# Both MLP products of a tuned fp32 encoder block by one level of Strassen's algorithm

## The chip, the cores and the metric

The kernel runs on one core of one Trainium2 chip. The metric is device microseconds (us) of one execution. The kernel before takes 1759.4 us in the median of three runs (1758.09 to 1764.33). One more execution was recorded by the profiler, and every time below that isn't such a run's comes from that record, counted from the start of its span.

## The reference, cut to what matters

The reference is one layer of an encoder on 1024 tokens of 1024 features: input projection, a state-space mixer, a neighbourhood attention, an output projection, and then the part that the change touches, a squared-ReLU MLP with 4096 hidden features, everything in float32:

```python
x = x + jnp.concatenate([y_ssm, y_na.astype(y_ssm.dtype)], axis=-1) @ w_out
h = rmsnorm(x, norm_mlp_w)
return x + jnp.square(jax.nn.relu(h @ w_mlp_in)) @ w_mlp_out
# x: (1, 1024, 1024), w_mlp_in: (1024, 4096), w_mlp_out: (4096, 1024)
```

## The kernel before

Each float32 product is made of three matmuls on values split in two: a high part, which is the value copied to the matmul's type (ACT), and a low part, the difference from it (a subtraction on POOL or DVE). `mm3` (lines 176 to 179) issues high times high, high times low and low times high into one PSUM tile. `load_w` (lines 133 to 150) loads 128 x 1024 elements of a weight (`wraw`, 512 KB, issued on SP), copies the high part `wh` on ACT (line 147) and subtracts the low part `wl` (line 148) on the engine it is given: POOL everywhere in the MLP. `split_from_psum` (lines 181 to 188) does the same for what comes out of PSUM, on ACT (line 183) and DVE (line 184).

The stages follow one another: projections with the mixer, the attention with the output projection mixed into it, then the MLP (line 968 on). The attention stage ends in the last products of the output projection, whose sums `po` DVE adds into `x2` (line 795). `x2`, 8 tiles of 128 tokens x 1024, lies in SBUF throughout.

The MLP begins with the norm of each token tile t: a square and sum on ACT (line 983), the root on POOL (lines 200 and 201), the scaled tile `hn` on DVE (line 985), eight 128 x 128 transposes on PE (line 209), and the split into `h2h` and `h2l`. `hn` has two buffers, so tile t waits for the transposes of t-2. Then 8 blocks `fb` of 512 hidden features. In a block, 4 columns j by 2 token halves h sum 8 parts k by three matmuls (192 of 128x512); each sum goes through relu (ACT, line 1011), square (DVE, 1012), and a split into `ah` (ACT, 1013) and `al` (DVE, 1014), which stay in SBUF. The block's part of the second product follows at once: 2 halves of the output by 8 token tiles by 4 parts by three matmuls (192 again), each sum added into `x2` on DVE (line 1024). In the last block each finished 128 x 512 piece goes out by DMA (line 1026).

The order on each engine comes from a scheduler that places instructions by estimated times when the program is built; each engine then works through its own list in that order, and an instruction that waits holds what stands behind it on its engine. DMAs are issued from such a list too (SP's).

## Time and profile before

| | us |
|---|---|
| runs, median (lowest to highest) | 1759.4 (1758.09 to 1764.33) |
| profiled execution, its span | 1754.2 |
| median of the runs less that span | 5.2 |
| PE busy in the span | 1695.5 (97%) |
| DVE, ACT, POOL busy | 948.8 (54%), 601.9 (34%), 555.1 (32%) |
| first matmul of the MLP, end of the last add | 1050.47, 1751.07 |

PE is TensorE's matmul stream, DVE VectorE, ACT ScalarE, POOL GpSimd and SP the engine that issues most DMAs. Busy time of PE is no measure of one matmul here, since matmuls overlap in its pipeline: the distance between starts is. The MLP takes the last 700 us of the span.

### The profile page before, as it was taken

To read this page: it belongs to the slowest core of one execution; us is meant where nothing else is said; L and a number is where in the kernel's file an instruction comes from. 1 tells how busy PE (TensorE), PEld (TensorE's weight loads), DVE (VectorE), ACT (ScalarE), POOL (GpSimd) and SP (SyncE) were. 2 spreads that over 40 slices of the span, in tenths; PEclk is the share of its full clock that TensorE was granted. 3 is DMA by queue.
4 is the path that set the end of the run, shared out by engine and by line. 5 is a ranking of instruction groups with operands and counts; after the bars stand their busy time and mean duration, and the time that the engine had idled before them with its cause. 6 is when DMAs were issued, how large, how long until landed. Compare 5 with 4: busy or idle time off the path is not lost.

```text
span 1754.2 us, 20790 instructions
## 1 busy us (share of the span) xinstructions
PE 1695.5 (97%) x7789; PEld 1368.8 (78%) x7789; DVE 948.8 (54%) x1601; ACT 601.9 (34%) x1079; POOL 555.1 (32%) x448
## 2 busy tenths in 40 slices
PE   6999999999898999999999999999999999999999
PEld 5788887777676777777777788888888888888887
DVE  4767115889787744787787745333333333333232
ACT  5434223334334433555565434131212121212120
POOL 4000005787788722220243124121212121212110
PEclk9999999999999999999999999999999999999999
DMA  8114239867676796563562112121212121212102
GB/s 208 49 39 121 72 97 259 205 177 225 200 211 180 230 286 208 190 192 94 167 205 85 49 48 84 49 60 37 61 37 60 37 61 37 60 37 60 37 13 96
DMA packets 176448, 202.63 MB, mean 116 GB/s; under 512 B 11915, under 2 KB 119387, under 8 KB 176347
## 3 DMA queue, kind: packets, MB, share of 16 engines
q1 hardware_dynamic: 133371, 164.07, 31.9%
q10 hardware_dynamic: 42976, 37.23, 7.0%
q8 instruction: 62, 1.02, 0.2%
q14 instruction: 39, 0.32, 0.1%
HBM read 151.66 MB, written 52.94 MB: 117 GB/s over the span
## 4 chain that ended last, share of the span: by engine, by line
PE 74%; DMA 7%; DVE 6%; POOL 6%; issue 4%; ACT 1%; SPq 1%; ACTq 0%; POOLq 0%; DVEq 0%
PE pm L178 13%; PE pm L179 13%; PE pm L177 13%; PE po L177 4%; PE po L179 3%; PE po L178 3%; PE pv L867 3%; PE px L177 3%; PE px L178 3%; PE px L179 3%; DMA rb<-cum_dr 2%; PE psc L893 2%; PE ptp L921 2%; POOL rb L611 2%; PE pz L179 2%
## 5 line engine op out<-in xcount | busy, mean ns | idle before, releaser
L148 POOL TENSOR_TENSOR wl<-wraw,wh 128x1024 fp32r<-128x1024 f32 x84 | 202.6, 2424 | 626.0 <-ACT wh L147 626.0
L147 ACT ACTIVATE wh<-wraw 128x1024 fp32r<-128x1024 f32 x124 | 131.1, 1059 | 407.8 <-PE pm L179 250.8
L1024 DVE TENSOR_TENSOR x<-x,pm 128x512 f32<-128x512 f32 x128 | 87.9, 687 | 230.8 <-PE pm L179 230.0
L178 PE MATMUL pm<-h2l,wh 128*128 128x512 f32 x512 | 199.4, 389 | 0.2 <-DVE h2l L184 0.2
L177 PE MATMUL pm<-h2h,wh 128*128 128x512 f32 x512 | 199.4, 389 | 0.0
L179 PE MATMUL pm<-h2h,wl 128*128 128x512 f32 x512 | 199.2, 389 | 0.0
L178 PE MATMUL pm<-wl,ah 128*128 128x512 f32 x512 | 199.2, 389 | 0.0
L179 PE MATMUL pm<-wh,al 128*128 128x512 f32 x512 | 199.2, 389 | 0.0
L177 PE MATMUL pm<-wh,ah 128*128 128x512 f32 x512 | 199.2, 389 | 0.0
L1012 DVE TENSOR_TENSOR r<-r 128x512 f32<-128x512 f32 x64 | 98.4, 1539 | 182.3 <-ACT r L1011 182.3
L178 PE MATMUL pq<-wl,hTh 128*128 128x512 f32 x384 | 153.5, 401 | 5.0 <-DVE wl L148 5.0
L177 PE MATMUL pq<-wh,hTh 128*128 128x512 f32 x384 | 154.7, 405 | 1.3 <-ACT wh L147 1.3
L179 PE MATMUL pq<-wh,hTl 128*128 128x512 f32 x384 | 153.1, 400 | 0.0
L178 PEld LDWEIGHTS pm<-h2l,wh 128*128 128x128 f32 x512 | 96.1, 188 | 20.5 <-DVE h2l L184 0.5
L177 PEld LDWEIGHTS pm<-wh,ah 128*128 128x128 f32 x512 | 96.1, 188 | 20.0
L177 PEld LDWEIGHTS pm<-h2h,wh 128*128 128x128 f32 x512 | 96.1, 188 | 19.9
L178 PEld LDWEIGHTS pm<-wl,ah 128*128 128x128 f32 x512 | 96.1, 188 | 19.9
L179 PEld LDWEIGHTS pm<-wh,al 128*128 128x128 f32 x512 | 96.1, 188 | 19.9
L179 PEld LDWEIGHTS pm<-h2h,wl 128*128 128x128 f32 x512 | 96.1, 188 | 19.8
L148 DVE TENSOR_TENSOR wl<-wraw,wh 128x1024 fp32r<-128x1024 f32 x40 | 55.1, 1382 | 80.0 <-ACT wh L147 79.3
L183 ACT ACTIVATE pth<-ptp 128x384 fp32r<-128x384 f32 (+1 forms) x128 | 58.5, 459 | 107.3 <-PE ptp L921 106.4
L178 PEld LDWEIGHTS pq<-wl,hTh 128*128 128x128 f32 x384 | 74.1, 193 | 22.3 <-DVE wl L148 7.6
(215 smaller groups left out, 3500.1 us busy)
## 6 DMA issues: line engine op xcount, KB each, us to landing
wraw<-in_w_in_dram SPq DMA_DIRECT2D x44, 512.0 KB, 4.3
rb<-cum_dr SPq DMA_DIRECT2D x32, 512.0 KB, 7.0
wraw<-in_w_mlp_in_dram SPq DMA_DIRECT2D x32, 512.0 KB, 4.2
wraw<-in_w_mlp_out_dram SPq DMA_DIRECT2D x32, 512.0 KB
q_dr<-hl ACTq DMA_DIRECT2D x64, 128.0 KB, 4.0
k_dr<-hl ACTq DMA_DIRECT2D x16, 512.0 KB, 3.2
v_dr<-hl ACTq DMA_DIRECT2D x16, 512.0 KB, 2.6
q<-q_dr SPq DMA_DIRECT2D x8, 1024.0 KB, 7.1
```

The lines of the kernel that those rows point to most:

```text
L147: nc.scalar.activation(hi[:, 0:n], raw[:, 0:n], AF.Copy)
L148: lo_eng.tensor_tensor(lo[:, 0:n], raw[:, 0:n], hi[:, 0:n].bitcast(F32), op=sub)
L177: nc.tensor.matmul(pt, lhsT=ah, rhs=bh, start=first, stop=False)
L178: nc.tensor.matmul(pt, lhsT=ah, rhs=bl, start=False, stop=False)
L179: return nc.tensor.matmul(pt, lhsT=al, rhs=bh, start=False, stop=last)
L183: nc.scalar.activation(hi, src, AF.Copy)
L611: nc.gpsimd.tensor_tensor(rb[:, d], rb[:, d], c1[:, d, c, h0 : h0 + 4].unsqueeze(2).broadcast_to([P, 4, P]), op=sub,)
L867: pvm = nc.tensor.matmul(pv[i][:, (c0 - 4 * i) * P : (c1 - 4 * i) * P], lhsT=v[:, g, hh], rhs=pt[:, g, c0 - g + 1 : c1 - g + 1, :], start= ...
L893: mark = nc.tensor.matmul(pt[:, 0:n], lhsT=q[hp, hh, qs], rhs=kl[hp, ks], start=False, stop=True)
L921: nc.tensor.transpose(pp[:, s], pr[:, s], ident)
L1012: nc.vector.tensor_tensor(r, r, r, op=mul)
L1024: nc.vector.tensor_tensor(d, d, pt, op=add)
```

## The change

Strassen's algorithm (Winograd's form) multiplies two matrices cut into 2 x 2 quarters with seven products of quarters for eight, at the price of sums and differences of quarters before and after. Here both MLP products are done so, and the MLP falls into two stages.

Stage 1 (8 blocks of 512 hidden features): the weight block is loaded in four quarters, combined on DVE (`s1w`, `s2w`, two differences) and split as before into `wh` and `wl` (ACT and POOL). The normed activations are combined once, at the stage's start (`b11` to `b22`, DVE on 2048 columns, then split into `hh` and `hl`). Seven products of 24 matmuls each, in the order 1, 2, 6, 5, 7, 3, 4, make the quarters `c11` to `c22` in SBUF, partly by ACT copies out of PSUM and partly by DVE adds; relu and square are on ACT. The seven combinations that the second product needs (`s1`, `s2`, `s4` among them) are stored to HBM as `act_dr`. `x2` is stored to HBM too.

Stage 2 (4 blocks of 1024 hidden features): weights are loaded, combined and split, the stored combinations are loaded (`ar`), split (`ah` on ACT, `al` on DVE), and seven products of 48 matmuls per block are added into `acc`, which is loaded from the stored `x2`.

The new functions `chain` (three matmuls, as `mm3`), `split_to` and `ring_tile` (buffers in a ring) are in the diff, which is cut to its core:

```diff
+    def split_to(hl, src, eng):
+        nc.scalar.activation(hl[0], src, AF.Copy)
+        eng.tensor_tensor(hl[1], src, hl[0].bitcast(F32), op=sub)
...
+        raws, hls = [wp] * 2 + [wq] * 6, [wp] * 3
...
             for t in range(NT):
                 xt = x2[:, t, :]
+                nc.sync.dma_start(x2_dr[t], xt)
...
                 nc.vector.scalar_tensor_tensor(hn, xt, r, wb, op0=mul, op1=mul)
-                transpose_split(h2h, h2l, t, hn)
...
+                    if i:
+                        split_from_psum(hc[i][0][s], hc[i][1][s], pv)
+                    nc.scalar.copy(xq[g, t // 4][s], pv)
...
+        def h_sub(out, a, b, i, eng):
+            nc.vector.tensor_tensor(out, a, b, op=sub)
+            if i:
+                hc_tiles(hB, i)
+                split_to(hc[i], out, eng)
+
+        b11, b12, b21, b22 = xq[0, 0], xq[0, 1], xq[1, 0], xq[1, 1]
+        h_sub(b11, b12, b11, None, None)
+        h_sub(b12, b22, b12, None, None)
+        h_sub(b22, b22, b11, 6, nc.vector)
+        hc_tiles(hB, 5)
+        split_to(hc[5], b11, nc.gpsimd)
+        hc_tiles(hB, 7)
+        split_to(hc[7], b12, nc.vector)
+        h_sub(b21, b21, b22, 4, nc.gpsimd)
...
+            for i in ORD:
+                if i == 1:
+                    w[1] = w_split(a11, nc.gpsimd)
+                    w[2] = w_split(a12, nc.gpsimd)
+                    s1w, s2w = raw_tile(), raw_tile()
+                    nc.vector.tensor_tensor(s1w, a21, a22, op=add)
+                    nc.vector.tensor_tensor(s2w, s1w, a11, op=sub)
+                    nc.vector.tensor_tensor(a21, a11, a21, op=sub)
+                elif i == 6:
+                    w[6] = w_split(s2w, nc.gpsimd)
+                    nc.vector.tensor_tensor(a12, a12, s2w, op=sub)
...
+                    if i in (1, 6, 5):
+                        nc.scalar.copy({1: c11, 6: c12, 5: c22}[i][:, j], pt)
+                    elif i == 4:
+                        nc.scalar.activation(c21[:, j], pt, AF.Relu)
+                    else:
+                        c = {2: c11, 7: c22, 3: c12}[i][:, j]
+                        nc.vector.tensor_tensor(c, c, pt, op=add)
...
+                elif i == 4:
+                    nc.scalar.activation(c21, c21, AF.Square)
+                    store(2, c21)
+                    nc.vector.tensor_tensor(s4, c21, s2, op=sub)
+                    store(3, s4)
...
+        raws, hls = [wp] * 2 + [wy] * 10, [wp] * 3 + [wy] * 3
...
+        def a_split(fb, i, u):
+            ar = ap2.tile([P, 1024], F32, tag="ar", name="ar", bufs=4)
+            nc.sync.dma_start(
+                ar.rearrange("p (a t) -> p a t", a=2), act_dr[fb, i - 1, :, 2 * u : 2 * u + 2, :]
+            )
+            hl = [ap2.tile([P, 1024], F32R, tag=n, name=n, bufs=5) for n in ("ah", "al")]
+            split_to(hl, ar, nc.vector)
+            return hl
...
+            for i in ORD:
+                wa = []
+                for u in range(2):
+                    q = bq[u]
+                    if i == 6:
+                        q["t1"], q["t2"] = raw_tile(), raw_tile()
+                        nc.vector.tensor_tensor(q["t1"], q["12"], q["11"], op=sub)
+                        nc.vector.tensor_tensor(q["t2"], q["22"], q["t1"], op=sub)
+                        nc.vector.tensor_tensor(q["12"], q["22"], q["12"], op=sub)
+                    elif i == 4:
+                        nc.vector.tensor_tensor(q["21"], q["21"], q["t2"], op=sub)
+                    src = q[{1: "11", 2: "21", 3: "22", 4: "21", 5: "t1", 6: "t2", 7: "12"}[i]]
+                    wa.append((a_split(fb, i, u), w_split(src, nc.gpsimd)))
...
+                    nc.vector.tensor_tensor(d, d, pt, op=add)
+                    if fb == 3 and i in (2, 7, 3, 4):
                         nc.sync.dma_start(
```

Up to the MLP the two programs issue the same instructions in the same order on every engine. PE's list is 384 matmuls shorter: 1344 in each stage, 2688 in all, for 3072.

The first place is DVE's list at the MLP's start. Before, the norm (`hn`, line 985) and the splits of the transposed tiles (`h2l`, line 184) are all that stands between the output projection's adds and the first block's squares:

```order
L985 SCALAR_TENSOR_TENSOR hn<-x_5436,r_9127,wb_9038 128x1024
L795 TENSOR_TENSOR x_5436<-x_5436,po 128x512
L184 TENSOR_TENSOR h2l<-ptn,h2h 128x4x128 x4
L985 SCALAR_TENSOR_TENSOR hn<-x_5436,r_9148,wb_9038 128x1024
L985 SCALAR_TENSOR_TENSOR hn<-x_5436,r_9169,wb_9038 128x1024
L184 TENSOR_TENSOR h2l<-ptn,h2h 128x4x128 x2
L985 SCALAR_TENSOR_TENSOR hn<-x_5436,r_9190,wb_9038 128x1024
L184 TENSOR_TENSOR h2l<-ptn,h2h 128x4x128 x4
```

Now (line numbers of the changed kernel: 1044 is `hn`, 1116 the last of four weight combinations, 1062 the combinations of activations, 994 a split's low part, `hl_9254` that of product 7 and `hl_9246` that of product 6; PE takes product 6 fourth here, after 1, 2 and 5):

```order
L1116 TENSOR_TENSOR wraw<-wraw 128x1024
L1044 SCALAR_TENSOR_TENSOR hn<-x_5436,r_9175,wb_9051 128x1024
L184 TENSOR_TENSOR hl_9043<-ptn,hh_9042 128x4x128 x2
L1044 SCALAR_TENSOR_TENSOR hn<-x_5436,r_9197,wb_9051 128x1024
L1044 SCALAR_TENSOR_TENSOR hn<-x_5436,r_9219,wb_9051 128x1024
L184 TENSOR_TENSOR hl_9043<-ptn,hh_9042 128x4x128
L1062 TENSOR_TENSOR xq<-xq 128x2048
L184 TENSOR_TENSOR hl_9043<-ptn,hh_9042 128x4x128
L1062 TENSOR_TENSOR xq<-xq 128x2048 x2
L994 TENSOR_TENSOR hl_9254<-xq,hh_9253 128x2048
L1062 TENSOR_TENSOR xq<-xq 128x2048
L994 TENSOR_TENSOR hl_9246<-xq,hh_9245 128x2048
```

From the last add of the output projection to `hl_9246`, DVE's list now has 12 splits of transposed tiles, 4 weight combinations, 4 `hn`, 4 combinations of activations and 2 splits of these, the last six of them 2048 wide.

The second place is DVE's list where stage 1 hands over to stage 2. Before, at the border of two blocks, the adds into `x2` are followed by the next block's squares and splits:

```order
L1024 TENSOR_TENSOR x_5436<-x_5436,pm_9690 128x512
L1024 TENSOR_TENSOR x_5436<-x_5436,pm_9704 128x512
L1024 TENSOR_TENSOR x_5436<-x_5436,pm_9718 128x512
L1012 TENSOR_TENSOR r<-r 128x512
L1014 TENSOR_TENSOR al<-r,ah 128x512
```

Now (1153 is the last combination of stage 1, `s4`; 1201 to 1205 are stage 2's combinations of weights; 994 is the first `al`):

```order
L1153 TENSOR_TENSOR cq<-cq 128x1024
L1201 TENSOR_TENSOR wraw<-wraw 128x1024
L1202 TENSOR_TENSOR wraw<-wraw 128x1024
L1203 TENSOR_TENSOR wraw<-wraw 128x1024
L1201 TENSOR_TENSOR wraw<-wraw 128x1024
L1205 TENSOR_TENSOR wraw<-wraw 128x1024
L1202 TENSOR_TENSOR wraw<-wraw 128x1024
L1203 TENSOR_TENSOR wraw<-wraw 128x1024
L994 TENSOR_TENSOR al<-ar,ah 128x1024
L1205 TENSOR_TENSOR wraw<-wraw 128x1024
L994 TENSOR_TENSOR al<-ar,ah 128x1024 x4
```

Seven combinations stand between `s4` and the first low part of a stored activation.

The third place is SP's list there, which issues the DMAs. Before, the MLP's list is nothing but weight loads, four by four:

```order
L146 DMA wraw<-in_w_out_dram 128x2x512
L146 DMA wraw<-in_w_mlp_in_dram 128x8x128 x4
L146 DMA wraw<-in_w_mlp_out_dram 128x2x512 x4
L1026 DMA out_dram<-x_5436 128x512 x16
```

Now (1097 are stores of combinations, 1184 weight loads of stage 2, 1194 the loads of `x2`, 1169 the loads of stored combinations):

```order
L1194 DMA acc<-x_dr 128x1024 x8
L1097 DMA act_dr<-cq 128x1024
L1184 DMA wraw<-in_w_mlp_out_dram 128x2x512
L1097 DMA act_dr<-cq 128x1024
L1184 DMA wraw<-in_w_mlp_out_dram 128x2x512 x2
L1097 DMA act_dr<-cq 128x1024 x2
L1184 DMA wraw<-in_w_mlp_out_dram 128x2x512
L1097 DMA act_dr<-cq 128x1024
L1184 DMA wraw<-in_w_mlp_out_dram 128x2x512 x3
L1169 DMA ar<-act_dr 128x1024 x4
```

The first load of a stored combination now stands behind the last store of stage 1 and three weight loads.

## Rows read from the trace of the kernel before

**Rows 1.** The page's busy times: engine, busy us, share, instructions.
```profile
PE 1695.5 (97%) x7789; PEld 1368.8 (78%) x7789; DVE 948.8 (54%) x1601; ACT 601.9 (34%) x1079; POOL 555.1 (32%) x448
```
**Rows 2.** The page's chain that ended last: shares by engine, then by line.
```profile
PE 74%; DMA 7%; DVE 6%; POOL 6%; issue 4%; ACT 1%; SPq 1%; ACTq 0%; POOLq 0%; DVEq 0%
PE pm L178 13%; PE pm L179 13%; PE pm L177 13%; PE po L177 4%; PE po L179 3%; PE po L178 3%; PE pv L867 3%; PE px L177 3%; PE px L178 3%; PE px L179 3%; DMA rb<-cum_dr 2%; PE psc L893 2%; PE ptp L921 2%; POOL rb L611 2%; PE pz L179 2%
```
**Rows 3.** End of that chain, from 1745 us: start, us, what.
```profile
1750.11 0.24 PE pm L179
1750.35 0.02 issue
1750.38 0.69 DVE x L1024
```
**Rows 4.** Windows: busy us (x instructions) of PE, PEld, DVE, ACT, POOL; PEclk, DMA share, GB/s.
```profile
1100.00:1700.00 600.00, 600.00 (x2649) 497.00 (x2648) 200.27 (x222) 121.46 (x163) 129.79 (x55) 1.00 0.15 46
```
**Rows 5.** Groups by line and shape, 1040 to 1760: count, busy us, mean ns, idle before.
```profile
L177 PE MATMUL pm<-h2h,wh 128*128 128x512 f32 x512 | 199.4, 389 | 0.0
...
L148 POOL TENSOR_TENSOR wl<-wraw,wh 128x1024 fp32r<-128x1024 f32 x63 | 151.6, 2418 | 485.6 <-ACT wh L147 485.6
...
L1024 DVE TENSOR_TENSOR x<-x,pm 128x512 f32<-128x512 f32 x128 | 87.9, 687 | 230.8 <-PE pm L179 230.0
L147 ACT ACTIVATE wh<-wraw 128x1024 fp32r<-128x1024 f32 x63 | 66.8, 1062 | 344.6 <-PE pm L179 250.8 <-PE pm L178 88.8 <-PE po L179 2.7
...
L1011 ACT ACTIVATE r<-pm 128x512 f32<-128x512 f32 x64 | 37.7, 590 | 62.9 <-PE pm L179 62.9
```
**Rows 6.** Single lines on DVE: duration ns min/median/max, first and last start.
```profile
L148 DVE TENSOR_TENSOR wl<-wraw,wh x40: 1161/1225/2303, 46.9 to 640.6; 128x1024 fp32r<-128x1024 f32 x40
```
**Rows 7.** The same for the MLP's norm on DVE (line 985).
```profile
L985 DVE SCALAR_TENSOR_TENSOR hn<-x,r,wb x8: 1274/1284/3406, 1031.4 to 1062.3; 128x1024 f32<-128x1024 f32 x8
```
**Rows 8.** The same for the MLP's squares on DVE (line 1012).
```profile
L1012 DVE TENSOR_TENSOR r<-r x64: 683/695/2503, 1068.8 to 1707.5; 128x512 f32<-128x512 f32 x64
```
**Rows 9.** PE at the border to the MLP: start, us, engine, line, operation.
```profile
1048.44 0.39 PE L179 MATMUL po<-wh,yl 128*128 128x512 f32 x1
1048.67 1.91 PE L209 MATMUL ptn<-ident,hn 128*128 128x128 f32 x16
1050.47 0.49 PE L177 MATMUL pm<-h2h,wh 128*128 128x512 f32 x1
```
**Rows 10.** DVE's last add of the output projection.
```profile
1048.87 0.69 DVE L795 TENSOR_TENSOR x<-x,po 128x512 f32<-128x512 f32 x1
```
**Rows 11.** POOL in the MLP, 1238 to 1263.
```profile
1239.98 2.39 POOL L148 TENSOR_TENSOR wl<-wraw,wh 128x1024 fp32r<-128x1024 f32 x1 [7.25 <-ACT wh L147]
```
**Rows 12.** DVE in the same stretch.
```profile
1240.42 2.50 DVE L1012 TENSOR_TENSOR r<-r 128x512 f32<-128x512 f32 x1 [4.07 <-ACT r L1011]
...
1245.15 0.69 DVE L1012 TENSOR_TENSOR r<-r 128x512 f32<-128x512 f32 x1 [0.84 <-ACT r L1011]
```
**Rows 13.** POOL at the MLP's start.
```profile
1050.01 2.40 POOL L148 TENSOR_TENSOR wl<-wraw,wh 128x1024 fp32r<-128x1024 f32 x1 [2.79 <-ACT wh L147]
...
1055.59 5.72 POOL L148 TENSOR_TENSOR wl<-wraw,wh 128x1024 fp32r<-128x1024 f32 x2
```
**Rows 14.** DVE in the same stretch.
```profile
1050.44 1.29 DVE L184 TENSOR_TENSOR h2l<-ptn,h2h 128x512 fp32r<-128x512 f32 x2 [0.89 <-ACT h2h L183]
...
1055.66 3.41 DVE L985 SCALAR_TENSOR_TENSOR hn<-x,r,wb 128x1024 f32<-128x1024 f32 x1 [0.72 <-POOL r L201]
```
**Rows 15.** PE in the mixer, after waits, 288 to 294.
```profile
291.12 0.63 PE L178 MATMUL pq<-wl,hTh 128*128 128x512 f32 x1
291.55 0.63 PE L179 MATMUL pq<-wh,hTl 128*128 128x512 f32 x1
```
**Rows 16.** The window around it, columns as in rows 4.
```profile
288.00:292.00 4.00, 4.00 (x15) 3.42 (x15) 3.50 (x9) 1.07 (x2) 1.96 (x2) 0.50 0.79 233
```
**Rows 17.** DMA issues in the MLP: count, KB each, median us to landing.
```profile
wraw<-in_w_mlp_in_dram SPq DMA_DIRECT2D x29, 512.0 KB, 4.2
out_dram<-x SPq DMA_DIRECT2D x16, 256.0 KB, 2.0
```
**Rows 18.** DMA issues in the attention stage, 600 to 1040.
```profile
k<-k_dr SPq DMA_DIRECT2D x16, 512.0 KB, 10.3
```

More of the change, by code (lines that the diff above doesn't have):

```diff
@@ L731, in hymba_block @@
                     nc.scalar.dma_start(v_dr[b, :, 8 * g : 8 * g + 8], hl.bitcast(F32))
[L736 removed]
+    x2s = ExitStack()
+    x2p = x2s.enter_context(tc.tile_pool(name="x2p", bufs=1, reuse_waits="tile"))
     x2 = x2p.tile([P, NT, D], F32, name="x2")
@@ L965, in hymba_block, with chain, ring_tile, raw_tile @@
         fill(-1)
-    with ExitStack() as ph:
-        h2 = ph.enter_context(tc.tile_pool(name="h2", bufs=1, reuse_waits="tile"))
-        h2h = h2.tile([P, KD, T], F32R, name="h2h")
-        h2l = h2.tile([P, KD, T], F32R, name="h2l")
-        enter_phase(ph, 3, 4, 3)
+    ORD = (1, 2, 6, 5, 7, 3, 4)
+    def chain(pt, ah, al, bh, bl, first, last):
+        for a, b, f, l in ((ah, bh, first, False), (ah, bl, False, False), (al, bh, False, last)):
+            nc.tensor.matmul(pt, lhsT=a, rhs=b, start=f, stop=l, skip_group_check=True)
+    ring = {"raw": 0, "hl": 0}
+    def ring_tile(key, pools, tags, dts):
+        n = ring[key]
+        ring[key] += 1
+        pool = pools[n % len(pools)]
+        return [
+            pool.tile([P, 1024], d, tag=t, name=t, bufs=pools.count(pool))
+            for t, d in zip(tags, dts)
+        ]
+    def split_to(hl, src, eng):
+        nc.scalar.activation(hl[0], src, AF.Copy)
+        eng.tensor_tensor(hl[1], src, hl[0].bitcast(F32), op=sub)
+    x2_dr = dr.tile([NT, P, D], F32, name="x2_dr")
+    act_dr = dr.tile([4, 7, P, 4, 512], F32, name="act_dr")
+    with ExitStack() as ph:
+        phase["ps"] = ph.enter_context(
+            tc.tile_pool(name="ps3", bufs=1, space=PSUM, reuse_waits="tile")
+        )
+        phase["mm"] = 4
+        hq, wq, hA = (
+            ph.enter_context(tc.tile_pool(name=n, bufs=1, side="right", reuse_waits="tile"))
+            for n in ("hq", "wq", "hA")
+        )
+        raws, hls = [wp] * 2 + [wq] * 6, [wp] * 3
+        def raw_tile():
+            return ring_tile("raw", raws, ("wraw",), (F32,))[0]
+        def w_split(src, eng):
+            hl = ring_tile("hl", hls, ("wh", "wl"), (F32R, F32R))
+            split_to(hl, src, eng)
+            return hl
+        hc = {}
+        def hc_tiles(pool, i):
+            hc[i] = [
+                pool.tile([P, 4, 512], F32R, tag=f"{n}{i}", name=f"{n}{i}") for n in ("hh", "hl")
+            ]
+        for i in (1, 2, 3):
+            hc_tiles(hA, i)
+        xq = {
+            (g, th): hq.tile([P, 4, 512], F32, tag="q", name="xq", bufs=4)
+            for th in range(2)
+            for g in range(2)
+        }
         with ExitStack() as p0:
@@ new lines, in hymba_block @@
+                for g in range(2):
+                    pt = (ps_tp if g else ps_s)("ptn")
+                    for j in range(4):
+                        k = 4 * g + j
+                        nc.tensor.transpose(
+                            pt[:, j * P : (j + 1) * P], hn[:, k * P : (k + 1) * P], ident
+                        )
+                    pv = pt.rearrange("p (j t) -> p j t", j=4)
+                    s = (slice(None), slice(None), slice(t % 4 * P, t % 4 * P + P))
+                    i = {(0, 0): 1, (1, 0): 2, (1, 1): 3}.get((g, t // 4))
+                    if i:
+                        split_from_psum(hc[i][0][s], hc[i][1][s], pv)
+                    nc.scalar.copy(xq[g, t // 4][s], pv)
@@ new lines, in hymba_block @@
+        x2s.close()
+        hB = ph.enter_context(tc.tile_pool(name="hB", bufs=1, reuse_waits="tile"))
+        def h_sub(out, a, b, i, eng):
[8 more added lines that the diff above has]
+        hc_tiles(hB, 5)
```

134 lines of the change are left out of this document (98 added, 36 removed).

## The prediction

> **What bounds the kernel now.** I read the page's busy times first: PE is busy for 97% of the span and no other engine for more than 54% [rows 1]. The chain that ended last says whether that share lies on the path: 74% of the span is PE's own, and its three largest lines, 13% each, are the MLP's matmuls (tile pm) [rows 2]. The end of that chain shows the exit: the last matmul, one DVE add of 0.69 us, and 3.1 us of output DMA up to the span's end at 1754.2 [rows 3]. Then the stage itself, in windows: from 1100 to 1700 PE is busy in all of the 600 us, with the clock granted in full (1.00, the 2.4 GHz level), while DVE works 200, ACT 121, POOL 130, and DMAs move 46 GB/s [rows 4]. So the MLP, from 1050.47 [rows 9] on, is bound by the number of matmuls and by nothing else. A group's mean of 389 ns [rows 5] is no price, since matmuls overlap; 600 us over 2649 matmuls give 0.2265 us for each.
>
> **What the change removes.** 384 of 3072 matmuls: 384 x 0.2265 = 87.0 us, if PE stays as closely fed as now. The shapes stay (128x512, three per term), and so does the exit after the last matmul. What is left to find is where PE will not be fed. Three places have to be looked at: the steady course of both stages, the start, and the switch between the stages.
>
> **Steady course.** A block of stage 1 has 168 matmuls, 38.05 us. POOL does seven low parts of 2.42 [rows 5], 16.9. DVE does eight sums of 1024 columns with both inputs in SBUF, at 1.23 (the median of the same shape [rows 6]), 9.8, and six adds out of PSUM at 0.69, 4.1. ACT does seven copies of 1.06, six evacuations and two relus of 0.59, and seven passes over 1024 (1.06), 19.6. DMAs: four loads and seven stores of 0.524 MB, 5.8 MB or 151 GB/s. A product of stage 2 has 48 matmuls, 10.87 us: POOL 4.8; DVE two low parts (2.45), 8/7 combinations (1.4) and four adds (2.75), 6.6; ACT 4.2; DMA 3.14 x 0.524 MB, again 151 GB/s. The windows show 233 GB/s moved in a stretch at 0.79 of the DMA engines [rows 16]. Each engine alone has room, and walking the built order with these durations I find every operand ready at least 3.5 us ahead of its product, so I cost the steady course at nothing. Its cover is that lead; without it see the second rival.
>
> One thing spoils the sum by engines. POOL and DVE do not always run at once. A low part on POOL starts at 1239.98 for 2.39 [rows 11]; the square that DVE starts at 1240.42 takes 2.50 and ends just after it, while the next takes 0.69 [rows 12]. The median of those squares is 695 ns, their longest 2503 [rows 8]. The norm's `hn`, normally 1.28, takes 3.41 [rows 7, 14] beside two low parts that together take 5.72 for 4.8 [rows 13]. But two splits whose source is PSUM take 1.29 beside a low part on POOL, as ever [rows 13, 14]. So DVE's operations with two inputs in SBUF, or SBUF throughout, wait for POOL's and POOL's for them, and the change makes many more of these.
>
> The Trainium skill says why, on its page "SBUF — State Buffer", section "Who interferes with whom": a DVE instruction with both inputs in SBUF and a GpSimd instruction that reads SBUF need one shared port pair, which one of them holds for its whole length, and a DVE instruction with at most one SBUF input is not concerned. The two squares of rows 12 (2.50 and 0.69 us) and the splits of rows 14 (1.29) agree. By the rule all the combinations and low parts of both stages exclude POOL's; by engine shares alone they would not, and the second rival below would have nothing to go by.
>
> **The start.** Before, PE goes from the output projection's last matmul (1048.44) through 16 transposes straight into the MLP at 1050.47 [rows 9]. In the changed order product 6, the fourth that PE takes, needs the low part `hl_9246`, which stands on DVE behind 12 splits out of PSUM (0.645 each, 7.7), 4 weight combinations (4.9), 4 `hn` (5.1), 4 combinations of activations and 2 low parts of 2048 columns (6 x 2.45 = 14.7). These 32.4 us start when the last add ends, at 1049.56 [rows 10]; without any wait `hl_9246` is there at 1082.0. There are waits: the first weight combination waits for loads that SP issues behind seven stores of `x2`; the last `hn` wait for transposes of tiles 4 and 5, because `hn` has two buffers and PE issues those only after product 1. Walking the list by hand with these gives 1087.8. If POOL holds DVE up for all that POOL does in that stretch (three low parts of 2.42 and one of 2048 columns, 4.84, in all 12.1), it is 1099.9. After `hl_9246` four products of 24 follow, 21.75 us. Without loss block 0 would end at 1050.47 + 38.05 + 2.9 (24 transposes by the 16 in 1.91 [rows 9]) = 1091.4. So the start costs 12.3 us at least, 18.1 by the walk and 30.2 at most. In rows 13 and 14 a waiting DVE gets in after one POOL operation; half of the 12.1 is the nearest to that, and I take 24. The work before product 6 that covers the wait (products 1, 2 and 5, 16.3 us, and the transposes) is in it.
>
> **The switch.** Stage 2 reads from HBM what stage 1 has just stored, and its first product needs weights and activations that nothing has fetched ahead. Let T be the end of stage 1's last matmul. Two lists meet there. SP: the last store of stage 1 waits for a relu (0.59), a square on ACT (1.06, as the copy of the same size) and the combination `s4` (1.23), T + 2.9; only behind it and three weight loads comes the first load of `ar`. It lands 4.2 us after its issue if alone [rows 17], 10.3 in a crowd, as the attention's k loads of the same size do [rows 18]; sixteen transfers of 512 KB are due within 8 us, so it is a crowd. With a copy (1.06) and a low part (1.23): T + 9.4 to T + 15.5. DVE: behind `s4` stand seven weight combinations, 8.6, then the first low part: T + 12.7; the second half's low part and one more combination, T + 15.1; with POOL's five low parts in between (12.1), T + 27.2. Some 1.8 us of matmuls need no low part and run earlier. So PE loses 11 us at least (T + 12.7) and 25 at most; the queue and POOL both push to the upper end, and I take 22.
>
> **The clock.** After PE has waited, its matmuls start 0.43 apart (291.12 to 291.55 [rows 15]), where 0.2265 is normal, and the granted clock there is 0.50, the 1.2 GHz level, over the 4 us of the window [rows 16]. Ten to fifteen matmuls at 0.2 us more are 2 to 3 us: 2 at the start, 3 at the switch.
>
> **Sum.** 87.0 - 24 - 2 - 22 - 3 = 36 us. The span goes from 1754.2 to 1718.2. The runs' median is 5.2 us above the span before; with the same 5.2 the time is 1723. With the lowest costs (12.3 and 11, the clock at nothing) it would be 1696, with the highest (30.2, 25, 5) 1733.
>
> **Rivals.**
> First, the two junctions are nearly hidden: DVE and POOL interleave without cost, and the loads of the switch arrive as if alone. 18 and 13 us then, 2 for the clock: 1759.4 - 54 = 1705. For it: the splits beside POOL that lose nothing [rows 14]. Against: the combinations have no PSUM input.
>
> Second, stage 2 is bound by DVE and POOL together. If every combination and low part excludes POOL's work, DVE's list lasts 4.8 + 6.6 = 11.4 us per product against 10.87 on PE; over 28 products 15 us more, 1738. For it: the squares that wait their full length [rows 12], and that POOL never rests for long. Against: the four adds per product (2.75) may run beside POOL, as 0.69 in every case shows [rows 5], and leads of some products smooth the rest.
>
> Third, slower than before: the three block borders inside stage 2 stall as the switch does. At each border eight weight loads stand on SP ahead of the loads of `ar` and wait for buffers of the block before, and DVE has its seven combinations to do before the low parts of product 1. If each costs 22 us like the switch, that is 66 us: 1789. It turns the gain into a loss from 36/3 = 12 us per border. For it: the lists are the same as at the switch. Against: nothing has to be stored first, and by the order the last weight buffer comes free two products (21.7 us) before the block ends, which covers 10.3 us of landing and the combinations.
>
> That the change doesn't do what it says is excluded by PE's list, which has 384 matmuls fewer.
>
> **How the numbers follow.** What can be told from no change in this kernel is 0.5%, 8.8 us. The forecast has a chance of 0.53, the first rival 0.20, the second 0.19, the third 0.08. The forecast's own range is 1710 to 1733. Below, the range takes in the first rival's 1705 and 5 us for a start nearer to its floor, 1700; above, the second's 1738 and 8 of the 10 us that the highest junction costs would add to it, 1746. Faster by over 0.5% (below 1750.6): all of the first two cases and most of the second rival, 0.53 + 0.20 + 0.14 = 0.87; within 0.5%: the rest of the second and the shallow end of the third, 0.06; slower: 0.07.
>
> **What would show it.** In the changed profile PE's matmuls of 128x512 in the MLP number 2688 and stand 0.2265 apart within blocks, without idle time there. PE's idle time gathers in two stretches: about 1050 to 1095, released by DVE, and one of about 20 us near 1380 to 1410, released by DVE low parts or ACT copies of `ar` that waited for a DMA. DVE's 1024-wide operations show a median of about 1.25 and many near 3.5. The prediction is wrong if PE idles regularly inside stage 2 (second rival), if each of three borders there shows a gap over 10 us (third), or if the two gaps together are under 30 us (first).

## The result and the profile after

The changed kernel takes 1739.6 us in the median of four runs (1735.2 to 1741.6), beside 1758.7 of the kernel before: a ratio of 0.989 with a 95% interval of 0.987 to 0.992, some 19 us faster. The forecast was 1723 in a range of 1700 to 1746. Direction and range held; of the 36 us forecast, half came, and 1739.6 lies above the 1710 to 1733 that the forecast gave as its own range.

The page's busy times (answering [rows 1]) and its chain (answering [rows 2]):

```profile
PE 1631.3 (94%) x7405; PEld 1302.9 (75%) x7405; DVE 1091.6 (63%) x1659; ACT 731.2 (42%) x1191; POOL 714.4 (41%) x498
...
PE 18%; DVE 0%; issue 0%; DVEq 0%
PE px L979 10%; PE pz L979 5%; PE py L979 3%; DVE al L994 0%; DVE acc L1225 0%; DVE wraw L1203 0%; DVEq L994 0%
```

PE has 384 matmuls less, and its share has fallen by 3 points. The chain goes back over 18% of 1738.4 us, 313 us, and all of that is PE: followed from the end, stage 2 is PE without a break, back to a DVE low part (`al`) at the switch. Next, what PE waited for from 1040 on (us in total, times, longest; the first four of twelve lines):

```profile
PE px L979 <- ACT ah L993: 26.6, 1, 26.6
PE ptn L1049 <- DVE hn L1044: 4.9, 1, 4.9
PE px L979 <- DVE hl L184: 4.6, 1, 4.6
PE px L979 <- DVE hl L994: 4.1, 1, 4.1
...
```

One wait of 26.6 us, the switch, and eleven short ones, all but one at the start. The windows place them (columns as in [rows 4]):

```profile
1050.00:1100.00 50.00, 32.16 (x126) 23.96 (x126) 37.51 (x26) 30.46 (x46) 21.56 (x14) 0.79 0.20 63
...
1400.00:1450.00 50.00, 27.02 (x102) 21.44 (x103) 30.56 (x24) 16.79 (x17) 20.98 (x8) 0.69 0.84 303
```
```profile
1150.00:1380.00 230.00, 230.00 (x1003) 187.58 (x1001) 94.06 (x82) 110.75 (x132) 100.97 (x42) 1.00 0.41 142
1450.00:1700.00 250.00, 250.00 (x1094) 205.13 (x1093) 184.32 (x161) 87.22 (x90) 135.69 (x46) 1.00 0.41 137
```

From 1150 to 1380 and from 1450 to 1700, across all three block borders of stage 2, PE is busy throughout at the full clock. Yet 230 us over 1003 matmuls are 0.2293 each and 250 over 1094 are 0.2285, where 0.2265 was the price before [rows 4], counted in the same way.

The account, against 0.2265 per matmul, uses two durations. Stage 1 from the output projection's last matmul to its own last one (1048.70 to 1395.14) lasts 346.4; without loss it would be 1344 x 0.2265 + 2.0 + 2.9 for the transposes, 309.3. Stage 2 with the switch (to 1734.18) lasts 339.0 for 304.4. I call the excess the loss: 37.1 and 34.6. The slower pitch is 1344 x 0.0028 = 3.8 of the first and 1344 x 0.0020 = 2.7 of the second.

| us | forecast | measured |
|---|---|---|
| 384 matmuls fewer | 87.0 | 87.0 |
| start, with the clock | 26 | 33.3 |
| switch, with the clock | 25 | 31.9 |
| steady course | 0 | 6.5 |
| off the span | 36 | 15.3 (spans: 1754.2 - 1738.4 = 15.8) |

**The start.** DVE, POOL and ACT in the changed kernel, start, duration and, in brackets, the idle time ahead with its releaser (answering [rows 13, 14]; 1062 and 994 are the combinations and low parts of 2048 columns):

```profile
1083.30 8.62 DVE L1062 TENSOR_TENSOR xq<-xq 128x2048 f32<-128x2048 f32 x2 [1.85 <-ACT xq L1057]
1091.84 2.29 DVE L994 TENSOR_TENSOR hl<-xq,hh 128x2048 fp32r<-128x2048 f32 x1
1094.04 4.46 DVE L1062 TENSOR_TENSOR xq<-xq 128x2048 f32<-128x2048 f32 x1
1098.42 4.44 DVE L994 TENSOR_TENSOR hl<-xq,hh 128x2048 fp32r<-128x2048 f32 x1
```
```profile
1082.88 4.57 POOL L994 TENSOR_TENSOR hl<-xq,hh 128x2048 fp32r<-128x2048 f32 x1 [7.53 <-ACT hh L993]
1092.58 3.76 POOL L994 TENSOR_TENSOR wl<-wraw,wh 128x1024 fp32r<-128x1024 f32 x1 [5.13 <-ACT wh L993]
1096.78 3.93 POOL L994 TENSOR_TENSOR wl<-wraw,wh 128x1024 fp32r<-128x1024 f32 x1 [0.43 <-ACT wh L993]
```
```profile
1068.01 1.06 ACT L993 ACTIVATE wh<-wraw 128x1024 fp32r<-128x1024 f32 x1 [3.23 <-PE px L979]
...
1069.92 1.06 ACT L1042 ACTIVATE hn<-x 128x1024 f32<-128x1024 f32 x1
```

What DVE waited for from 1049.9 to 1102 (us in total, times, longest; two of four lines, the others are 2.3 and 1.3):

```profile
DVE hl L184 <- ACT hh L183: 5.7, 3, 3.6
DVE wraw L1111 <- DMA wraw<-in_w_mlp_in_dram: 3.2, 1, 3.2
```

Product 6's low part is the last DVE row: it ends at 1102.86, where my walk had 1087.8 and my ceiling 1099.9. Of the five operations shown, one keeps its 2.29 us; beside three POOL operations the others take 8.62 for 4.58, then 4.46 and 4.44 for 2.29 each, 8.4 us more. DVE's waits are the other part, 12.5 us, the longest for ACT. ACT's rows show why: the squares of the last two token tiles (the first at 1069.92) stand behind a `wh` copy that waits 3.23 us for PE, which no walk along DVE's list alone shows.

**The switch.** SP's issues (answering [rows 17, 18] with the order shown ahead of the prediction), then ACT's first `ah` and DVE's first weight combination:

```profile
1387.89 4.89 SPq L1194 DMA_DIRECT2D acc<-x_dr  x8
...
1405.15 7.36 SPq L1184 DMA_DIRECT2D wraw<-in_w_mlp_out_dram  x3
1412.55 1.89 SPq L1169 DMA_DIRECT2D ar<-act_dr  x4
```
```profile
1421.05 1.06 ACT L993 ACTIVATE ah<-ar 128x1024 fp32r<-128x1024 f32 x1 [2.22 <-DMA ar<-act_dr]
```
```profile
1409.57 2.50 DVE L1201 TENSOR_TENSOR wraw<-wraw 128x1024 f32<-128x1024 f32 x1 [11.06 <-DMA wraw<-in_w_mlp_out_dram]
```

The eight loads of `acc`, 4.2 MB, go out ahead of everything that product 1 needs. Then SP waits. A row of its list runs from the first issue to the end of the last, and the waits between them are in it: one weight load takes 0.38 us to issue, and most of the 7.36 us of three is waiting. What SP waited for from 1387 to 1430 (two lines of ten):

```profile
SPq L1184 <- DVE wraw L1201: 10.9, 2, 5.6
...
SPq L1097 <- DMA acc<-x_dr: 3.1, 4, 0.9
```

The first of the two waits for L1201, DVE's first weight combination, is 5.3 us long and stands ahead of the third of these loads; most other waits are for earlier transfers to land. The first `ar` is issued 17.4 us after stage 1's last matmul (1395.14). The DMA engines are full all the while:

```profile
1387.90:1421.05 33.15, 7.62 (x34) 5.91 (x32) 12.63 (x11) 8.38 (x10) 10.06 (x4) 0.68 1.01 367
```

That is a busy share of 1.01 at 367 GB/s, 12.2 MB up to the first `ah`. PE resumes at half clock:

```profile
1395.14 0.39 PE L979 MATMUL px<-hh,wl 128*128 128x512 f32 x1
1422.15 0.79 PE L979 MATMUL px<-wh,ah 128*128 128x512 f32 x1 [26.63 <-ACT ah L993]
1422.75 0.63 PE L979 MATMUL px<-wl,ah 128*128 128x512 f32 x1
1423.17 0.63 PE L979 MATMUL px<-wh,ah 128*128 128x512 f32 x1
```

### The profile page after: what moved, and what is told of

Same layout as the page of the kernel before. It is cut to its first block, busy times and chain, and to the rows that moved or that the text cites. A ratio compares the mean times of both kernels' runs of the same rounds, so it can differ in the third digit from the quotient of the medians.

```text
span 1738.4 us, 20791 instructions
## 1 busy us (share of the span) xinstructions
PE 1631.3 (94%) x7405; PEld 1302.9 (75%) x7405; DVE 1091.6 (63%) x1659; ACT 731.2 (42%) x1191; POOL 714.4 (41%) x498
## 5 line engine op out<-in xcount | busy, mean ns | idle before, releaser
L994 POOL TENSOR_TENSOR wl<-wraw,wh 128x1024 fp32r<-128x1024 f32 x112 | 303.9, 2724 | 332.6 <-ACT wh L993 321.1
L993 ACT ACTIVATE ah<-ar 128x1024 fp32r<-128x1024 f32 x56 | 58.9, 1053 | 187.4 <-PE px L979 99.1
L979 PE MATMUL px<-wh,ah 128*128 128x512 f32 x256 | 101.2, 395 | 26.6 <-ACT ah L993 26.6
L994 DVE TENSOR_TENSOR al<-ar,ah 128x1024 fp32r<-128x1024 f32 x56 | 105.4, 1886 | 31.5 <-ACT ah L993 29.9
L979 PE MATMUL px<-hl,wh 128*128 128x512 f32 x256 | 102.1, 399 | 8.7 <-DVE hl L184 4.6
L148 POOL TENSOR_TENSOR wl<-wraw,wh 128x1024 fp32r<-128x1024 f32 x20 | 48.6, 2445 | 141.2 <-ACT wh L147 141.1
L979 PE MATMUL px<-hh,wh 128*128 128x512 f32 x256 | 101.3, 397 | 2.8 <-ACT cq L1130 2.0
L979 PE MATMUL px<-wh,al 128*128 128x512 f32 x256 | 101.2, 397 | 0.8 <-DVE al L994 0.8
L979 PE MATMUL px<-wl,ah 128*128 128x512 f32 x256 | 101.9, 398 | 0.0
L979 PE MATMUL px<-hh,wl 128*128 128x512 f32 x256 | 101.2, 396 | 0.0
L177 PE MATMUL po<-wh,yh 128*128 128x512 f32 x208 | 87.1, 419 | 1.8 <-DVE x L796 1.8
L179 PEld LDWEIGHTS pq<-wh,hTl 128*128 128x128 f32 x384 | 74.3, 193 | 15.5
```

What stands on the lines that cost most here:

```text
L148: lo_eng.tensor_tensor(lo[:, 0:n], raw[:, 0:n], hi[:, 0:n].bitcast(F32), op=sub)
L177: nc.tensor.matmul(pt, lhsT=ah, rhs=bh, start=first, stop=False)
L179: return nc.tensor.matmul(pt, lhsT=al, rhs=bh, start=False, stop=last)
L979: nc.tensor.matmul(pt, lhsT=a, rhs=b, start=f, stop=l, skip_group_check=True)
L993: nc.scalar.activation(hl[0], src, AF.Copy)
L994: eng.tensor_tensor(hl[1], src, hl[0].bitcast(F32), op=sub)
```

## The experiments

Each ratio below is to the kernel before, measured beside it; the changed kernel has 0.989. "Loss" is as above, from one profiled execution each: 37.1 in stage 1 and 34.6 in the switch with stage 2. Where an edit leaves a stage alone, the first is 36.8 to 37.4 in the other executions (33.5 in e9, whose pools lie elsewhere) and the second 33.0 to 35.3, so that differences of 1 to 2 us say little.

**e1: the loads of `acc` behind the first product's loads.**

```diff
-            if fb == 0:
-                for t in range(NT):
-                    nc.sync.dma_start(acc[:, t, :], x2_dr[t])
+                if fb == 0 and i == 1:      # behind the last ar load of product 1
+                    with tc.issue_after(ld[0].ins):
+                        for t in range(NT):
+                            nc.sync.dma_start(acc[:, t, :], x2_dr[t])
```

> The eight loads of acc (4.2 MB) are issued behind the first two loads of stored combinations, instead of ahead of stage 2's weights. Theory (the switch waits for a saturated DMA queue): 4.2 MB at the 410 GB/s that the changed kernel's trace shows there are 10 us; PE's gap of 26.6 us at the switch shrinks to 15 to 18 us and the time falls by 8 to 11 us, to about 1730. Rival (DVE's seven weight combinations, beside POOL's low parts, set the end of the gap): the gap stays within 3 us and the time within 3 us of 1739.6.

Measured: 0.989 (0.987 to 0.990). The wait at the switch fell from 26.6 to 22.0, the loss from 34.6 to 31.2; a new wait of 2.2 for `ah` came in product 2. The first `ar` was issued at 1406.0, again behind three weight loads, of whose 7.19 us 5.3 are a wait for DVE's first combination. So `acc` carries a part of the switch, between the two expectations; stores and weights alone fill the DMA engines too (share 1.00 from stage 1's last matmul to the first `ah`).

**e2: all low parts of the start on DVE, none on POOL.**

```diff
-        split_to(hc[5], b11, nc.gpsimd)
+        split_to(hc[5], b11, nc.vector)
-        h_sub(b21, b21, b22, 4, nc.gpsimd)
+        h_sub(b21, b21, b22, 4, nc.vector)
+                    lo = nc.gpsimd if fb else nc.vector   # for w[1], w[2], w[6], ... of block 0
```

> At the start of stage 1 POOL's low parts (those of the first weight block and of two combinations of activations) are made by DVE, which so has about 6 us more of its own work ahead of product 6. Theory (DVE and POOL exclude each other, and DVE stood still for some 10 us of its own instructions there, 8.62 for two that take 4.5, 4.46 and 4.44 for two of 2.3): DVE's long instructions go back to 1.2 and 2.3 us, and the start gets 2 to 6 us shorter. Rival (the start is long by DVE's own work and the round trips to ACT and PE): 5 to 8 us longer.

Measured: 0.986 (0.984 to 0.987); loss of stage 1 30.3, 6.8 less, though DVE now does POOL's share as well. Its operations of 2048 columns are back to 2.29:

```profile
1085.24 2.29 DVE L1062 TENSOR_TENSOR xq<-xq 128x2048 f32<-128x2048 f32 x1
1087.44 2.29 DVE L994 TENSOR_TENSOR hl<-xq,hh 128x2048 fp32r<-128x2048 f32 x1
```

So the lengthening came from POOL. The exclusion is shown, and two engines that take turns are worth less here than one alone.

**e3: 24 matmuls without use between the stages, to hold the clock.**

```diff
+                for _ in range(24):
+                    nc.tensor.matmul(
+                        X[0], lhsT=ident, rhs=ident.unsqueeze(1).broadcast_to([P, 4, P]),
+                        start=True, stop=True,
+                    )
```

> 24 matmuls on the identity, whose results are overwritten, fill PE's gap at the switch. Theory (after the gap PE starts at half clock, 20 matmuls 0.43 apart): the granted clock stays at 1.00 there, the first product runs 0.23 apart, and the time falls by 3 to 5 us. Rival (the first product is fed by DVE's low parts, which come no earlier): PE waits in it instead, and the time moves by less than 1.5 us.

Measured: 0.991 (0.989 to 0.992), the loss 34.6 as before. The fillers and the first product, then the window of the first 16 matmuls in the changed kernel and in this one:

```profile
1393.06 20.76 PE L1197 MATMUL px<-ident 128*128 128x512 f32 x48
1419.86 0.80 PE L979 MATMUL px<-wh,ah 128*128 128x512 f32 x1 [6.03 <-ACT ah L993]
1420.45 0.63 PE L979 MATMUL px<-wl,ah 128*128 128x512 f32 x1
1420.88 0.63 PE L979 MATMUL px<-wh,ah 128*128 128x512 f32 x1
```
```profile
1422.20:1430.30 8.10, 7.27 (x16) 5.24 (x17) 8.10 (x6) 4.01 (x4) 3.35 (x2) 0.50 0.72 250
```
```profile
1419.90:1428.00 8.10, 7.26 (x16) 5.29 (x17) 8.10 (x6) 4.01 (x4) 3.36 (x2) 0.50 0.75 262
```

The edit did not do what it was made for. The fillers (24 in the program, 48 rows in the trace) end 6.03 us before the first product, which then runs at half clock (0.50, starts 0.43 apart) for 8.1 us in both kernels. So e3 decides neither the theory nor the rival: what half clock costs at the switch stays open. Sixteen matmuls at 0.2 us more are 3.2 us, the 3 that I set down; how much of that would be spent waiting for low parts at full clock no run shows.

**e4: the stores of `x2` issued by ACT, after the norm.**

```diff
-                nc.sync.dma_start(x2_dr[t], xt)
+        for t in range(NT):
+            nc.scalar.dma_start(x2_dr[t], x2[:, t, :])
```

> The stores of x2 are issued on ACT's list and no longer ahead of the first weight loads on SP's. Theory (the first weight combination and with it product 1 wait for loads that stand behind these stores): DVE's wait of 3.2 us and PE's of 4.6 us go, and the time falls by 2 to 4 us. Rival (the next wait, for the norm of tiles 4 to 7 and its transposes, takes it up): the time moves by less than 1.5 us.

Measured: 0.990 (0.988 to 0.991). The wait for `hl` fell from 4.6 to 2.1, the loss of stage 1 by 1.5 to 35.6. The first weight combination waits 1.1 us for its loads instead of 3.2, but most of that is taken up by later waits.

**e5: all tiles on the right side shifted by 64 bytes.** Products 1, 2 and 3 of stage 1 run at 0.2333 per matmul (median over six successive starts), 5, 6, 7 and 4 at 0.2267; the first group reads activations that lie on the right side of SBUF, the second on the left. The kernel before has 0.2267 by its starts too (2647 in 600 us) and stage 2 has 0.2289; the windows' 0.2265 and 0.2285 are a little lower, since a window counts the matmuls that straddle its edges.

```diff
+        pd.tile([P, 16], F32, tag="pad", name="pad", bufs=1)    # ahead of hq, wq, hA
+        pd.tile([P, 16], F32, tag="pad", name="pad2", bufs=1)   # ahead of ap2
```

> Nothing but 64 bytes of unused SBUF in front of the tiles on the right side: the activations of products 1 to 3 of stage 1, which had started 0.2333 us apart where products 4 to 7 took 0.2267, and the activations of stage 2 (0.2289) now begin at a multiple of 128 bytes plus 32, as those of products 4 to 7 and of the kernel before do, and no longer plus 96. Theory (the address within 128 bytes sets the pace): all pitches become 0.2267, and the time falls by 5 to 8 us. Rival (it is the side of SBUF, or the product, and not the offset): pitches and time unchanged within 2 us.

Measured: 0.993 (0.991 to 0.995). The theory fell. Stage 1 kept both pitches, and stage 2 became slower:

```profile
1450.00:1700.00 250.00, 250.00 (x1073) 201.14 (x1072) 179.95 (x157) 86.68 (x89) 129.83 (x44) 1.00 0.40 133
```

250 over 1073 are 0.2330, for 0.2285. Where a tile lies does matter, since nothing else was edited, but not by the rule that I had in mind.

**e6: product 6's weight combinations behind the first low parts on DVE.**

```diff
+                        with ExitStack() as late:
+                            if fb == 0 and u == 0:
+                                late.enter_context(tc.issue_after(al_ins[0]))
                             nc.vector.tensor_tensor(q["t1"], q["12"], q["11"], op=sub)
```

> Product 6's weight combinations in stage 2's first block are put behind the first four low parts of stored combinations on DVE. Theory (DMAs set the gap at the switch, DVE only what comes next): the gap stays at 25 to 27 us, and 1 to 3 us are won after it. Rival (the seven combinations on DVE set it, as the prediction had half of it): the gap falls to 15 to 19 us and the time by 8 or more.

Measured: 0.989 (0.986 to 0.991); the wait at the switch is 25.6 for 26.6, the loss 31.9, 2.7 less.

```profile
1404.67 18.58 SPq L1173 DMA_DIRECT2D ar<-act_dr  x8
```
```profile
1416.80 1.06 ACT L995 ACTIVATE ah<-ar 128x1024 fp32r<-128x1024 f32 x1 [11.11 <-DMA ar<-act_dr]
```

SP's wait for DVE is gone from the way to the first `ar`, which is issued 12.7 us after stage 1's last matmul (1391.95) for 17.4. Yet its copy begins at 24.9 for 25.9: the DMA engines stay full, and the load takes the longer to land. The seven combinations on which my 12.7 us rested hide behind the transfers: the switch waits for DMAs, not for DVE.

**e7: the switch reordered.** e1 and e6, weights loaded in the order of their use, and the pools of stage 1 exchanged, so that stage 2's first buffers come free earlier.

```diff
-        hq, wq, hA = (
+        hA, wq, hq = (
-                bq.append({n: raw_tile() for n in ("11", "21", "12", "22")})
+            for n in ("11", "21", "12", "22"):
+                for u in range(2):
+                    bq[u][n] = raw_tile()
```

> Four edits at the switch: the activations' pool comes first on the right side of SBUF, so that stage 2's buffers lie where products 1 and 2 of stage 1 are done early; the two buffers that are free ahead hold the two weights of product 1; acc is loaded behind the first loads of stored combinations; product 6's combinations stand behind the first low parts. Theory (the gap is the time from the last store's queue and the freed buffers to the first operands, so loads that can start ahead of the end of stage 1 close it): the gap falls from 26.6 to under 10 us and the time by 15 to 25 us, to 1715 to 1725. Rival (DMA bandwidth: stores, weights and stored combinations don't fit whatever their order): the gap stays above 17 us, and the time falls by less than 9.

Measured: 0.984 (0.982 to 0.986). Stage 2's first matmul follows 0.22 us after stage 1's last, but the wait comes back at the fourth product:

```profile
PE px L979 <- DVE acc L1237: 19.1, 1, 19.1
```

`acc`, now loaded last, holds PSUM tiles that product 6 needs. The loss is 24.6, 10 less. The gap closed as the theory had it, but the gain is 9.5 us by the ratios and not 15 to 25: most of the wait was moved.

**e8: the start.** e2, e4 and eight buffers for the norm's tile.

```diff
-                hn = np_.tile([P, D], F32, tag="hn", name="hn")
+                hn = np_.tile([P, D], F32, tag="hn", name="hn", bufs=8)
```

> Three edits at the start: eight buffers for hn instead of two (all norms run as soon as their tile is summed), the first block's low parts on DVE, the stores of x2 on ACT's list. Theory (the start is a chain: hn's buffers, transposes behind product 1, copies, then combinations held up by POOL): stage 1's loss against 0.2265 per matmul falls from 37 to 18 to 26 us and the time by 11 to 19. Rival (DVE's and ACT's own work, some 40 us each for the first block, sets the start): it falls by no more than the 7 us that moving the low parts alone gave.

Measured: 0.979 (0.977 to 0.981); loss of stage 1 19.7, 17.4 less, within the theory's range. The three alone gave 6.8, 1.5 and, in e10, 4.7, 13.0 in all; that the three together are worth more isn't shown, since the same edits take 14.3 off in e11. The switch is as before (26.4). The longest wait left at the start is 4.4, for a copy out of PSUM (`xq`).

**e9: the switch, second try.** e6 and e7's order of weights; the first two products' `ar` ahead of the weights, which need their pools placed so that they are free; `acc` in two tiles, each loaded between weights.

```diff
+            pre = {(i, u): a_split(0, i, u) for i in (1, 2) for u in range(2)} if fb == 0 else {}
+                    if fb == 0 and n == "12" and u == 0:
+                        with tc.issue_after(lx.ins):
+                            for t in range(4):
+                                lw = nc.sync.dma_start(acc[0][:, t, :], x2_dr[t])
```

> The switch again, with acc's first half ahead of the late weights: the buffers of stage 2's first two products lie where products 1 to 3 of stage 1 (and its weights) are done early, acc is two tiles, its first half behind product 2's weights and ahead of product 6's, its second half last; ah and al have four buffers each. Theory (what closed the gap but turned into a 19 us wait of product 6 for adds into acc was the place of acc's loads in the queue, 4.2 MB behind all else): no wait over 10 us is left at the switch, and the time falls by 18 to 27 us against the changed kernel, to a ratio to the kernel before of 0.974 to 0.979. Rival (8 to 9 MB have to pass at 410 GB/s before product 6 in any order, so the wait is only moved): 15 us or more are still lost, the ratio is 0.982 to 0.985, as in the last try.

Measured: 0.981 (0.978 to 0.983); loss of the switch with stage 2 18.7, 16 less, with 10.3 us of waiting for weights in product 6, in two waits. No single wait is over 10 us, as the theory had it, but the gain, 15 us by the ratios, is short of its 18, and more than the rival's 15 us are still lost.

**e10: eight buffers for `hn` alone**, the edit shown under e8.

> Of the three edits at the start only the eight buffers for hn. The three together took 17 us from stage 1, low parts on DVE alone 7, the stores alone 1.5. Theory (the norm's round trip through two buffers is the larger part): 6 to 10 us faster than the changed kernel, ratio about 0.984 to 0.986. Rival (DVE's standstill beside POOL takes back what the norm gives while the low parts are still on POOL): 0 to 4 us, ratio 0.987 to 0.989.

Measured: 0.986 (0.983 to 0.989); loss of stage 1 32.4, 4.7 less. The wait for `hn` is gone, waits for `xq` (8.0 in four pieces) and for product 6's low part (5.0) stand in its place. By the ratios 5.6 us are won, between theory and rival.

**e11: e8 and e9 together.**

> The three edits at the start and the second switch together. If the two losses are independent, their gains add up: 18 to 19 at the start and 18 to 27 at the switch, so 1739.6 becomes 1694 to 1703, a ratio to the kernel before of 0.963 to 0.969. Rival (both are held by the same thing, DVE and POOL over the whole stage, so one gain hides the other): less than 30 us together, a ratio above 0.972.

Measured: 1710.1 us, 0.974 (0.972 to 0.977), losses of 22.8 and 17.7. It beats both kernels: by the ratios 45 us under the one before and 26 under the changed one. The theory's 0.963 to 0.969 is missed, and the number falls to the rival (above 0.972, less than 30 us). By the losses 31.2 us are gone where e8 and e9 took 17.4 and 15.9, so that the rival's reason, one gain hiding the other, is hardly borne out. Its longest wait, and SP's list around it:

```profile
PE pz L979 <- ACT wh L995: 9.2, 1, 9.2
```
```profile
1388.27 8.95 SPq L1175 DMA_DIRECT2D ar<-act_dr  x3
1397.31 2.05 SPq L1196 DMA_DIRECT2D acc<-x_dr  x4
```

6.1 of the 8.95 us of the three `ar` are two waits for DVE's low parts (`al`), the rest waits for earlier transfers: the issue itself takes 0.32 us.

**e12: that list reordered, and all tiles shifted by 32 bytes.**

```diff
+                if fb == 0 and i == 6:
+                    late.enter_context(tc.issue_after(last_w[0]))
                 nc.sync.dma_start(
                     ar.rearrange("p (a t) -> p a t", a=2),
-        rcol = cp.tile([P, NT], F32, name="rcol")
+        rcol = cr.tile([P, NT], F32, name="rcol")    # cr: a pool on the right side
```

> The kernel of e11 with two more edits that are read at different places. First: product 6's four loads of ar go behind the last weight load of the first block, so that the loads of acc follow the last stores at once. Theory: e11's wait of 9.2 us ahead of product 6's tail came from SP's list (three loads of ar stood 8.95 us in front of the loads of acc and of the last weights); the wait falls under 3 us and the switch with stage 2 loses about 10 us instead of 17.7. Rival: the DMA engines carry 8 to 9 MB there at about 410 GB/s whatever the order, and the wait stays within 3 us of 9.2. Second: every SBUF tile is shifted by 32 bytes (one small tile goes from the left side to the right), so that all matmul operands, which begin 32 bytes past a multiple of 64 so far, begin at a multiple of 64; the order on every engine is the same. Theory: the pitches of 0.2333 and 0.2289 come from operands that begin off such a boundary, so all products go to 0.2267 or below, a block of stage 1 takes 38.1 us instead of 38.6, a product of stage 2 10.9 instead of 10.99, and the span falls by some 7 us more. Rival: the side on which a tile lies decides, or something finer; the pitches stay at 0.2267, 0.2333 and 0.2289. Time by both theories 1694, by the first alone 1702, by none 1710; ratio to before 0.965, 0.970, 0.974.

Measured: 0.979 (0.977 to 0.981), slower than e11 by 8 us; of the 14.3 us between the two profiled executions 5.7 lie ahead of the MLP, whose start ranges from 1044 to 1053 over all of them. Both theories fell. The wait ahead of product 6 did not shrink but grew to 19.4, now for `ah`, and the loss of the switch went from 17.7 to 27.8:

```profile
PE px L979 <- ACT ah L995: 19.4, 1, 19.4
```
```profile
1400.16 4.00 SPq L1216 DMA_DIRECT2D acc<-x_dr  x4
1405.07 4.20 SPq L1178 DMA_DIRECT2D ar<-act_dr  x4
```
```profile
1396.00:1420.00 24.00, 9.94 (x44) 7.82 (x42) 18.57 (x15) 4.26 (x5) 11.19 (x5) 0.81 1.03 412
```
```profile
1450.00:1700.00 250.00, 250.00 (x1094) 205.13 (x1093) 187.26 (x162) 88.07 (x90) 131.98 (x44) 1.00 0.40 134
```

The engines moved 412 GB/s over those 24 us, so whatever goes first delays the rest: the rival was right that the order only moves the wait, though not that its size stays. The last row has 1094 matmuls again, as in the changed kernel, and stage 1 keeps its 0.2267 and 0.2333: a shift of all operands by 32 bytes changes no pitch.

## Why the prediction was right, and where its sizes were off

**The mechanism and the sign held.** PE bounds the MLP, 384 matmuls at 0.2265 went, and PE idles at the two junctions that the prediction named, released by DVE and by ACT copies of late `ar` loads. The second rival is refuted by the windows: no idle time in stage 2 beside 184 us of DVE and 136 of POOL in 250. The third is refuted by the same row, which spans the three borders. The first rival, junctions nearly hidden, is refuted by 33 and 32 us for its 18 and 13. The exit is as before (4.2 us from the last matmul's start to the span's end), and DVE's operations of 1024 columns are of two kinds as foretold, though fewer come near 3.5: of 56 `al`, 1.89 us in the mean, 31 take 1.21 to 1.23 and 25 take 2.69 to 2.85.

**The range held by luck in part.** All three terms of the loss came out higher than forecast: 20.7 us in all, and the two junctions together above even their highest costs with the clock (65.2 for 60.2). The forecast's own range ended at 1733. That 1739.6 lies within the stated one is due to the room left for the second rival, whose 1738 is near in number and wrong in mechanism. And a part of the miss cancelled: I added 5.2 us for the runs above the profiled span, but this time the median lies only 1.2 above it.

**The start: a term of 26 that measured 33.3.** The chain was the right one: `hl_9246` is there at 1102.86, 9 us after the 1093.8 that my 24 stand for. Two steps along DVE's list were too small. I charged half of POOL's 12.1 us on the ground that a waiting DVE gets in after one operation. It does, but only to meet the next one: in the last six operations alone 8.4 us were lost, and one `hn` took 2.96 for 1.28, 10.0 in all for 6. The Trainium skill, "SBUF — State Buffer", section "Who interferes with whom", calls the port pair that DVE and GpSimd share an exclusive lock; 8.62 for two operations of 2.29 beside one of 4.57 agrees. And the waits in DVE's list are 12.5 us, where the walk had 5.8 (1087.8 less 1082.0): it left out that ACT's squares and splits stand behind a copy waiting for PE. PE itself is slow there, with a clock of 0.79 in the window: eleven matmuls after 1060.7 at 0.43, and sixteen transposes in 3.36 us for 1.91 [rows 9]. What that adds to the waits, for which I put 2, no run separates. The two buffers of `hn`, which the walk had as a wait, are worth 4.7 (e10).

**The switch: a term of 25 that measured 31.9.** The step that failed is "sixteen transfers of 512 KB are due within 8 us", for which I charged a landing of 10.3 us behind an issue at T + 2.9. The eight loads of `acc`, which stand first in the order shown, were not in that count: up to the fourth `ar` SP issues 24 transfers (8 `acc`, 7 weights, 5 stores, 4 `ar`), and the 12.2 MB that move up to the first `ah` are 23 of them. Nor did I divide volume by rate: at 0.37 MB per us even sixteen take 23 us. So the first `ar` went out some 17 us after T, and its copy began 26 after it. My other chain took DVE as the bound; e6 shows that DVE hardly counts (1.0 of the wait), e1 that `acc` does (4.6), e9 that order and buffers together give 16. That volume bounds the switch is the reading that fits all of these; e1 wins less than the 11 us that 4.2 MB take, since 2.3 MB move under stage 1's last matmuls in the changed kernel (323 GB/s in the 7.24 us before its end, 77 in e1). The Trainium skill, "DMA: Bandwidth & Descriptors", section "Where 436 GB/s comes from", puts the ceiling of the fabric at 435 GB/s and the HBM limit per core at about 358; the 412 of e12 stay under the first and are over the second. The clock's 3 us are untested (e3).

**The steady course: a term of 0 that measured 6.5.** Every operand was ready in time, as the walk said; the matmuls themselves got slower, by 0.9% in stage 2 and 1.2% in stage 1, where four of seven products keep the price of before and three don't. I took the price of a matmul for a constant of its shape. e5 changes stage 2's by moving the right side's tiles by 64 bytes and leaves stage 1's as they were, e12 changes none by moving all tiles by 32; what decides stays open.

## What to carry to other kernels

Where PE is the bound and work is taken from it, price the places where it starts and restarts by the whole volume that is due there: every transfer on the queue, whoever needs it, at the rate at which the full DMA engines move it. A row of the issuing engine that looks like slow issue can be waiting: its waits tell for what. Work that DVE and POOL both do out of SBUF was nearer to a sum than to a maximum here, so at a start on the critical path one of the two alone may be quicker (e2). And a mean over a window doesn't show that an edit took hold where it was meant to: look at the matmuls themselves (e3).

## What the runs showed of the hardware

- The same 128x512 matmul, fed without idle time at the full clock, took 0.2267 us from start to start before, and 0.2267, 0.2289 or 0.2333 after by the product; 64 bytes of shift on one side moved stage 2 from 0.2289 to 0.2333 and stage 1 not, 32 bytes for all tiles moved nothing.
- With the DMA engines full (share 1.01 to 1.03), loads and stores together went at 367 GB/s over 33 us and at 412 over 24 us.
- DVE's operations of 2048 columns out of SBUF took 2.29 us, two of them 8.62 and single ones 4.44 and 4.46 beside POOL's; with POOL's low parts moved to DVE they were back at 2.29 (e2).
- After 20.8 us of fillers at a granted clock of 1.00 and 6.03 us without a matmul, PE's next 16 matmuls ran at 0.50, the lower of its two levels (e3).
